# Two-layer diffusion trunk on one core: where mask additions and a modulation part stand, and how many chunks go stream by stream

## The chip, the cores and the metric

The kernel runs on one core of a Trainium2 chip. The metric is the device time of one execution in microseconds (us); less is better. The core's engines each run their own fixed instruction stream: TensorE (PE in the profile, its weight loads PEld), VectorE (DVE), ScalarE (ACT), GpSimd (POOL) and SyncE (SP), which here only issues DMAs. An engine waits at an instruction until the semaphores it names have arrived, and everything behind that instruction on the engine waits with it.

## The reference

512 tokens of width 1024, 256 of them context and 256 latent (a grid of 4 rows by 64), go through two layers, all in fp32. Cut to what matters here:

```python
mod = silu(c) @ w_ada[l] + b_ada[l]          # 6 parts: sh1, sc1, gt1, sh2, sc2, gt2 (latent; the same for context)
h = rms_norm(x, g_attn[l]) * (1 + sc1) + sh1
p = h @ w_in[l]                              # gates | c_q (768) | c_kv (256) | k_r (32) | neighbourhood q, k, v
mq = rms_norm(rms_norm(c_q) @ w_uq)          # 8 heads of 96; the last 32 are rotated (rope_2d)
kv = rms_norm(c_kv) @ w_ukv                  # 8 heads of 64 + 64
mk = rms_norm([k_nope, k_r]);  the k_r part is rotated
y_mla = softmax(mq mk') mv                   # latent queries over context + latent, context over context
y_na  = softmax(nq nk' + bias)               # 8 x 16 windows of the grid with rpb, and all context keys
x = x + gt1 * (sigmoid(g1) * (y_mla @ w_mla_o) + sigmoid(g2) * (y_na @ w_na_o)) @ w_out[l]
h2 = rms_norm(x, g_mlp[l]) * (1 + sc2) + sh2
x = x + gt2 * (relu(h2 @ w_ff1[l]) ** 2 @ w_ff2[l])
```

The output is the latent stream; so the second layer updates the latent tokens alone.

## The kernel before

**Products.** Every fp32 product is made of three TensorE products of values rounded to fp32r: `mm3` (L100 to L103) multiplies the high part of the weights with the high and with the low part of the activations (L101 and L102 or L103), and the low part of the weights with the high one. A weight block comes by DMA from SP's queue into one of five `raw` tiles (`wraw`, L116 to L122); `wsplit` (L124 to L129) makes `whi` of it on ACT (L127) and `wlo` on DVE (L128), into one of three pairs of tiles. `proj_a` (L131) takes the output features in chunks of 128: split, 24 matmuls over all 512 tokens, evacuation (`evac`), and then `step()`. `proj_tail` (L150) is for the last chunks of a product: it splits the weights of all of them, and then does the tokens of one stream (256 columns) for each chunk, and then the other stream's, so that the norm that follows can begin with the stream that is done first. In both `hook` is called ahead of each k of the eight.

**Modulation.** `ada_side` (L233) computes parts of the modulation without TensorE: a part `(l, j, zs)` is column block j of layer l's `w_ada` for the vectors zs. For each of 8 blocks of 128 rows it loads 512 KB (the `raw` ring, SP's queue) and adds the rows, times silu(c), into accumulators on DVE (L246 for the first block, L248 for the others: two vectors of 1024 columns, in halves of 512 in the part of layer 0's attention). Then come transposes and reductions on DVE, one small matmul and the biases. It is a generator; it stands in the list `side`, and `step(n)` (L163) advances it by n pieces. Part (0,2) is the first gate of layer 0. `step(2)` (L685), the evacuation of the w_uq product (L719), that of the w_ukv product (L737), and `step(99)` (L750), which does all that is left, advance it. The list of layer 0's feed-forward (L1232) begins with part (0,5) and is advanced by that block's chunks.

**Norms.** `rms_a` (L306): one column of sums by TensorE (L311), eps added by DVE (L316), and a power on POOL (L177) that gives `rt`. `rms_b` (L321) spreads it over the partitions (TensorE, L324). `norm_apply` (L330) then does one k of 8: DVE `u` (L334), ACT high part (L338), DVE low part (L340). `last_product` (L1068) is w_out of layer 0 (then norm 2) and the last eighth of w_ff2 of layer 0 (then norm 1 of layer 1): 6 chunks by `proj_a`, 2 by `proj_tail`, with `rms_a` for the first stream ahead of (1, 1, 0), that is second stream, second chunk, k 0, and its norm ahead of (1, 1, 5). The second stream's norm is in `ff1_hook` (L1119; ahead of the first stream's second and third chunk) and, at the start of layer 1, in `ckv_hook` (L515; k 4 and k 7 of the first c_kv product).

**Attention's preparation.** The w_uq product (three groups of heads) is evacuated by ACT into `mq` (L715) and its squares summed (L597); the w_ukv product into `mk` and `mv`. POOL then has in program order: `q_stat` (L694 and others), `k_stat` (L707 and the power L177), `k_fin` (to L745) for four blocks of tokens, and `q_fin` (L697), which scales the context queries' last 32 columns (L702) and rotates the latent ones by `rope` (L607 to L617). TensorE goes on with the gates (L756): 6 chunks in layer 0 and 8 in layer 1, and then transposes queries (L775) and keys (L780) for the first head. `prep_na` (L790) loads for each head of the neighbourhood part a bias tile by 4 DMAs on SP's queue (L809) and adds the mask to it on POOL (L810); there are three such tiles in layer 0 and four in layer 1.

**The order** on each engine is fixed when the kernel is built, by a list scheduler that takes what is ready by its model, by priority of program position: what stands later in the program can be hoisted ahead (mask additions and modulation pieces among it). `keep_in_program_order` pins an instruction. `tc.issue_after(i)` places what is traced in its block behind i on the same engine; it adds no semaphore.

Of the kernel before, what the change touches and what calls it, by code (L numbers as in the profile page):

```python
# [45 lines left out]
def trunk(ctx: ExitStack, tc, t):  # L46
# [186 lines left out]
    def ada_side(parts, acc):  # L233


        for l, j, zs in parts:
            accs = [acc(z) for z in zs]
            for k in range(KD):
                raw = wraw(t["w_ada"][l], k, 1, j * D, D)[:, 0]
                for z, tiles in zip(zs, accs):  # L240
                    sc = silu[:, k, z:z + 1]
                    c = 0
                    for a in tiles:
                        w = a.shape[-1]
                        if k == 0:
                            nc.vector.tensor_scalar(out=a, in0=raw[:, c:c + w], scalar1=sc, scalar2=None, op0=ALU.mult)  # L246
                        else:
                            nc.vector.scalar_tensor_tensor(out=a, in0=raw[:, c:c + w], scalar=sc, in1=a,  # L248
                                                           op0=ALU.mult, op1=ALU.add)
                        c += w  # L250
                yield
# [78 lines left out]
    def norm_apply(k, xT, R, A, SH, hh, hl, streams, half=False):  # L330

        u = sp.tile([128, TT], F32, tag="tmp", name="u", bufs=NTMP)
        for s, c in streams:
            nc.vector.scalar_tensor_tensor(out=u[:, c], in0=xT[:, k, c], scalar=A[:, k, s:s + 1],  # L334
                                           in1=R[:, :c.stop - c.start] if half else R[:, c],
                                           op0=ALU.mult, op1=ALU.mult)
        for s, c in streams:
            nc.scalar.activation(out=hh[:, k, c], in_=u[:, c], func=AF.Identity, bias=SH[:, k, s:s + 1])  # L338
        for s, c in streams:
            nc.vector.scalar_tensor_tensor(out=hl[:, k, c], in0=u[:, c], scalar=SH[:, k, s:s + 1],  # L340
                                           in1=hh[:, k, c].bitcast(F32), op0=ALU.add, op1=ALU.subtract)

# [114 lines left out]
    for l in range(DEPTH):  # L457
# [57 lines left out]
        def ckv_hook(k):  # L515

            if k == 4:
                nxt.append(rms_a(nxt[2], both[1][1], "C", True))
            if k == 7:
                nxt[3](1, rms_b(*nxt[4], True))  # L520
# [86 lines left out]
        def rope(z, tab, lt, n):  # L607
# [8 lines left out]
            for i in range(2):  # L616
                nc.gpsimd.tensor_tensor(out=zz[:, :, :, i], in0=aa[:, :, :, i], in1=bb[:, :, :, 1 - i], op=ALU.add)  # L617
# [63 lines left out]
        if l == 0:  # L681
            block_sum()
            side.append(ada_side(((0, 2, (0, 1)),), lambda z: [ap.tile([128, TT], F32, tag="P", name="ada", bufs=4)
                                                               for _ in range(2)]))
            step(2)  # L685
# [11 lines left out]
        def q_fin(tk):  # L697
            z = mq[:, tk, :, NOPE:QK]
            if tk >= 2:
                rope(z, ropeq[:, l], tk - 2, NH)  # L700
            else:
                nc.gpsimd.tensor_tensor(out=z, in0=z, in1=gqr[:, l, :].unsqueeze(1).to_broadcast([128, NH, RD]),  # L702
                                        op=ALU.mult)
# [8 lines left out]
        for h0, n in ((0, 3), (3, 3), (6, 2)):  # L712
            def evac(tk, o):
# [5 lines left out]
                if tk % 2:  # L719
                    step()  # L720
# [29 lines left out]
        step(99)  # L750
        for tk in range(4):
            k_fin(tk)
        for tk in range(q0, 4):
            q_fin(tk)

        gates(NG0[l], "B")  # L756

# [32 lines left out]
        def prep_na(hp):  # L790
# [12 lines left out]
            for h in (2 * hp, 2 * hp + 1):  # L803
                bias = ap.tile([128, 2, ROWS, GW], F32, tag="bias", name="bias", bufs=3 + l)
                for row in range(ROWS):
# [4 lines left out]
                nc.gpsimd.tensor_tensor(out=bias.rearrange("p a i j -> p (a i) j"),  # L810
                                        in0=bias.rearrange("p a i j -> p (a i) j"),
                                        in1=wmask.unsqueeze(1).to_broadcast([128, 2 * ROWS, GW]), op=ALU.add)
# [255 lines left out]
        def last_product(w, k0, moves, gate, acc, then):  # L1068
# [12 lines left out]
            def hook(s_, i, k):  # L1081

                if (s_, i, k) == (1, 1, 0):
                    Rs.append(rms_a(acc, both[0][1], "D", True))
                if (s_, i, k) == (1, 1, 5):
                    then(rms_b(*Rs[0], True))

            proj_a(w, k0, KD, 0, 6, moves, loc, res_add(gate, sq))
            proj_tail(w, k0, (6, 7), moves, both, ev, hook)
# [20 lines left out]
        def norm_2(i, R):  # L1110
            for k in range(KD):
                norm_apply(k, xT, R, A2[l], SH2, mh, ml, [streams[i]], True)
# [3 lines left out]
                          gained if last else lambda R: norm_2(0, R))  # L1116
        R2 = []

        def ff1_hook(f):  # L1119

            if f == 1:
                R2.append(rms_a(Rs, both[1][1], "C", True))
            if f == 2:
                norm_2(1, rms_b(*R2[0], True))
# [12 lines left out]
        def ff1(g):  # L1137
# [21 lines left out]
            if g == 0 and not last:  # L1159
# [3 lines left out]
                for s_, c in both:  # L1163
                    for f, (o, (h, lo)) in enumerate(zip(os, hls)):
                        if s_ == 0:
                            ff1_hook(f)
                        for k in range(KD):
                            mm3(o[:, c], h[:, k], lo[:, k], mh[:, k, c], ml[:, k, c], k == 0, k == KD - 1)
# [8 lines left out]
        def ff2(g, a):  # L1177
            if g == 3:
# [3 lines left out]
                def norm_1(i, R):  # L1182
                    for k in range(KD):
# [3 lines left out]
                                   lambda R: norm_1(0, R))  # L1187
# [44 lines left out]
        if l == 0:  # L1232
            side.append(ada_side(((0, 5, (0, 1)), (1, 1, (0, 1)), (1, 0, (0, 1)), (1, 2, (1,)), (1, 4, (1,)),
                                  (1, 3, (1,)), (1, 5, (1,))), acc_g))
# [67 lines left out]
```

## Time and profile before

| | |
|---|---|
| device time, median of 3 runs | 1317.09 us (1316.2 to 1318.02) |
| profiled execution, its own time | 1316.76 us |
| span of that execution in the trace | 1315.0 us (1.76 us lie around it) |
| mean granted TensorE clock | 0.992 of full speed |
| PE busy | 1276.4 us, 97% |
| DVE busy | 903.5 us, 69% |
| ACT busy | 582.6 us, 44% |
| POOL busy | 269.7 us, 21% |

Times are microseconds from the start of the span. A row names start, duration, engine, line, operation, tiles out and in, shape and count; the bracket behind it is the idle time of the engine ahead of it and what released it. "SPq" is a DMA issue on SP's queue.

### The profile page before, as it was taken

To read this page: it belongs to the slowest core of one execution; us is meant where nothing else is said; L and a number is where in the kernel's file an instruction comes from. 1 tells how busy PE (TensorE), PEld (TensorE's weight loads), DVE (VectorE), ACT (ScalarE), POOL (GpSimd) and SP (SyncE) were. 2 spreads that over 40 slices of the span, in tenths; PEclk is the share of its full clock that TensorE was granted. 3 is DMA by queue.
4 is the path that set the end of the run, shared out by engine and by line. 5 is a ranking of instruction groups with operands and counts; after the bars stand their busy time and mean duration, and the time that the engine had idled before them with its cause. 6 is when DMAs were issued, how large, how long until landed. Compare 5 with 4: busy or idle time off the path is not lost.

```text
span 1315.0 us, 20278 instructions
## 1 busy us (share of the span) xinstructions
PE 1276.4 (97%) x7783; PEld 1094.9 (83%) x7783; DVE 903.5 (69%) x1545; ACT 582.6 (44%) x1052; POOL 269.7 (21%) x283
## 2 busy tenths in 40 slices
PE   7989999999999999999999999989999999999997
PEld 5788888986787898888888888889889789999896
DVE  4588387758985597997775665756763967665553
ACT  4445376446423334322323313455654545554452
POOL 0325501421004003210201100038122112121011
PEclk9999999999999999999999999999999999999999
DMA  9865500544495336566675572476214657656652
GB/s 290 298 147 148 174 17 17 180 134 57 114 321 182 114 111 179 169 182 195 205 224 176 160 224 85 120 176 182 77 49 113 134 171 211 175 159 194 192 183 90
DMA packets 241857, 208.01 MB, mean 158 GB/s; under 512 B 24464, under 2 KB 220816, under 8 KB 241376
## 3 DMA queue, kind: packets, MB, share of 16 engines
q1 hardware_dynamic: 231728, 190.16, 50.3%
q10 hardware_dynamic: 9520, 16.29, 3.5%
q8 instruction: 61, 1.00, 0.3%
q0 software_dynamic: 512, 0.27, 0.1%
q14 instruction: 36, 0.29, 0.1%
HBM read 195.15 MB, written 11.53 MB: 157 GB/s over the span
## 4 chain that ended last, share of the span: by engine, by line
PE 55%; DVE 3%; DMA 2%; ACT 1%; POOL 1%; issue 1%; POOLq 0%; ACTq 0%; DVEq 0%
PE psB L101 7%; PE psB L103 7%; PE psB L102 7%; PE psA L103 6%; PE psA L101 6%; PE psA L102 6%; PE psC L103 4%; PE psC L101 4%; PE psC L102 4%; PE psC L865 1%; DVE wlo L128 1%; PE psD L885 1%; ACT whi L127 1%; DMA raw<-in_w_uq_dram 1%; DMA bias<-in_rpb_dram 1%
## 5 line engine op out<-in xcount | busy, mean ns | idle before, releaser
L128 DVE TENSOR_TENSOR wlo<-raw,whi 128x1024 fp32r<-128x1024 f32 (+3 forms) x252 | 308.5, 1226 | 190.9 <-ACT whi L127 185.4
L127 ACT ACTIVATE whi<-raw 128x1024 fp32r<-128x1024 f32 (+3 forms) x252 | 260.4, 1035 | 364.1 <-PE psB L102 113.8
L248 DVE SCALAR_TENSOR_TENSOR ada<-raw,silu,ada 128x1024 f32<-128x1024 f32 (+1 forms) x126 | 153.1, 1245 | 25.5 <-DMA raw<-in_w_ada_dram 25.2
L102 PE MATMUL psA<-wlo,h 128*128 128x256 f32 (+2 forms) x408 | 121.1, 297 | 2.5 <-DVE wlo L128 2.5
L101 PE MATMUL psA<-whi,h 128*128 128x256 f32 (+2 forms) x408 | 120.8, 296 | 1.2 <-ACT h L338 1.1
L103 PE MATMUL psA<-whi,h 128*128 128x256 f32 (+2 forms) x408 | 120.9, 296 | 0.0
L101 PE MATMUL psB<-h,whi 128*128 128x512 f32 (+1 forms) x288 | 99.1, 345 | 0.1
L103 PE MATMUL psB<-h,wlo 128*128 128x512 f32 (+1 forms) x288 | 99.0, 344 | 0.0
L102 PE MATMUL psB<-h,whi 128*128 128x512 f32 (+1 forms) x288 | 99.0, 344 | 0.0
L101 PE MATMUL psA<-h,whi 128*128 128x512 f32 (+1 forms) x248 | 87.8, 355 | 0.8 <-ACT h L338 0.8
L103 PE MATMUL psA<-h,wlo 128*128 128x512 f32 (+1 forms) x248 | 87.3, 352 | 0.0
L102 PE MATMUL psA<-h,whi 128*128 128x512 f32 (+1 forms) x248 | 87.1, 351 | 0.0
L102 PEld LDWEIGHTS psA<-wlo,h 128*128 128x128 f32 x408 | 78.4, 192 | 5.6 <-DVE wlo L128 3.1
L101 PEld LDWEIGHTS psA<-whi,h 128*128 128x128 f32 x408 | 78.1, 192 | 3.4 <-ACT h L338 1.6
L103 PEld LDWEIGHTS psA<-whi,h 128*128 128x128 f32 x408 | 78.2, 192 | 1.9
L1156 POOL TENSOR_TENSOR fl<-s,fa 128x512 fp32r<-128x512 f32 (+1 forms) x32 | 36.2, 1130 | 167.0 <-ACT fa L1155 167.0
L101 PE MATMUL psC<-G,whi 128*128 128x258 f32 (+2 forms) x216 | 69.2, 321 | 0.3 <-ACT G L338 0.3
L102 PE MATMUL psC<-G,whi 128*128 128x258 f32 (+2 forms) x216 | 69.1, 320 | 0.2
L103 PE MATMUL psC<-G,wlo 128*128 128x258 f32 (+2 forms) x216 | 68.8, 319 | 0.2 <-DVE wlo L128 0.2
L1156 POOL TENSOR_TENSOR h<-s,h 128x512 fp32r<-128x512 f32 (+1 forms) x32 | 34.5, 1077 | 168.3 <-ACT h L1155 150.0
L102 PEld LDWEIGHTS psB<-h,whi 128*128 128x128 f32 x288 | 54.6, 190 | 6.8 <-issue 0.8
L101 PEld LDWEIGHTS psB<-h,whi 128*128 128x128 f32 x288 | 54.6, 190 | 6.9 <-issue 0.4
(389 smaller groups left out, 3323.7 us busy)
## 6 DMA issues: line engine op xcount, KB each, us to landing
raw<-in_w_ff_dram SPq DMA_DIRECT2D x128, 512.0 KB, 4.1
raw<-in_w_ada_dram SPq DMA_DIRECT2D x80, 512.0 KB, 4.1
raw<-in_w_in_dram SPq DMA_DIRECT2D x62, 512.0 KB, 3.7
raw<-in_w_out_dram SPq DMA_DIRECT2D x16, 512.0 KB, 4.5
spare<-in_w_ada_dram SPq DMA_DIRECT2D x12, 512.0 KB, 8.6
xT_d<-xT SPq DMA_DIRECT2D x2, 2048.0 KB, 10.2
bias<-in_rpb_dram SPq DMA_DIRECT2D x64, 64.0 KB, 7.0
g_d<-g ACTq DMA_DIRECT2D x16, 256.0 KB, 4.4
```

Source lines behind the costliest of these rows:

```text
L101: nc.tensor.matmul(out, sh, mh, start=first, stop=False)
L102: nc.tensor.matmul(out, sh, ml, start=False, stop=False)
L103: nc.tensor.matmul(out, sl, mh, start=False, stop=last)
L127: nc.scalar.activation(out=hi, in_=src, func=AF.Copy)
L128: nc.vector.tensor_tensor(out=lo, in0=src, in1=hi.bitcast(F32), op=ALU.subtract)
L248: nc.vector.scalar_tensor_tensor(out=a, in0=raw[:, c:c + w], scalar=sc, in1=a, op0=ALU.mult, op1=ALU.add)
L865: nc.tensor.transpose(o[:, kt * 256 + i * 128:kt * 256 + (i + 1) * 128], pt[:, (kp * 2 + kt) * 128:(kp * 2 + kt + 1) * 128], perm if K == ...
L885: mm = nc.tensor.matmul(yo[z * 64:(z + 1) * 64, oc], vsel(kt, 2 * hp + z), tr[kt // 2][:, kt % 2, :], start=kt == nkt - 1, stop=kt == 0, t ...
L1156: nc.gpsimd.tensor_tensor(out=al[:, f, :], in0=s[:, :TQ], in1=ah[:, f, :].bitcast(F32), op=ALU.subtract)
```

## The change

- **Mask additions.** The addition of the mask to a bias tile (L810, both layers) is placed on POOL behind `q_end`, the last operation of the last query block's `q_fin`.
- **Modulation (0,2).** `step(2)` and the step in the w_uq evacuation go. The part is advanced by the w_ukv evacuations, by the gates' chunks, and the rest by `step(99)`, which now stands behind the gates.
- **Modulation (0,5) and those after it.** The first of these operations (L246) is placed on DVE behind the last operation of norm 2 of the second stream (`behind`, a function that gives that instruction).
- **Last products of layer 0.** 5 chunks by `proj_a` and 3 by `proj_tail`; `rms_a` ahead of (1, 0, 7); k 0 to 4 of the first stream's norm ahead of (1, 1, 4), and k 5 to 7 after the tail.
- **Second stream's norms.** `ckv_hook` at k 3 and 6 in place of 4 and 7; in ff1 `rms_a` ahead of (1, 0) as before and the norm ahead of (1, 5), in place of (2, 0).

```diff
-    def ada_side(parts, acc):
+    def ada_side(parts, acc, behind=None):
...
+                lead, behind = behind, None
...
                         if k == 0:
-                            nc.vector.tensor_scalar(out=a, in0=raw[:, c:c + w], scalar1=sc, scalar2=None, op0=ALU.mult)
+                            with tc.issue_after(lead()) if lead else nullcontext():
+                                nc.vector.tensor_scalar(out=a, in0=raw[:, c:c + w], scalar1=sc, scalar2=None,
+                                                        op0=ALU.mult)
...
-            if k == 4:
+            if k == 3:
                 nxt.append(rms_a(nxt[2], both[1][1], "C", True))
-            if k == 7:
-                nxt[3](1, rms_b(*nxt[4], True))
+            if k == 6:
+                nxt[3](1, rms_b(*nxt[4], True), range(KD))
...
             side.append(ada_side(((0, 2, (0, 1)),), lambda z: [ap.tile([128, TT], F32, tag="P", name="ada", bufs=4)
                                                                for _ in range(2)]))
-            step(2)
...
                 if h0 == 6:
                     q_stat(tk)
-                if tk % 2:
-                    step()
...
-        step(99)
         for tk in range(4):
             k_fin(tk)
         for tk in range(q0, 4):
-            q_fin(tk)
+            q_end = q_fin(tk)
 
         gates(NG0[l], "B")
+        step(99)
...
-                nc.gpsimd.tensor_tensor(out=bias.rearrange("p a i j -> p (a i) j"),
-                                        in0=bias.rearrange("p a i j -> p (a i) j"),
-                                        in1=wmask.unsqueeze(1).to_broadcast([128, 2 * ROWS, GW]), op=ALU.add)
+                with tc.issue_after(q_end.ins):
+                    nc.gpsimd.tensor_tensor(out=bias.rearrange("p a i j -> p (a i) j"),
+                                            in0=bias.rearrange("p a i j -> p (a i) j"),
+                                            in1=wmask.unsqueeze(1).to_broadcast([128, 2 * ROWS, GW]), op=ALU.add)
...
-                if (s_, i, k) == (1, 1, 0):
+                if (s_, i, k) == (1, 0, 7):
                     Rs.append(rms_a(acc, both[0][1], "D", True))
-                if (s_, i, k) == (1, 1, 5):
-                    then(rms_b(*Rs[0], True))
-
-            proj_a(w, k0, KD, 0, 6, moves, loc, res_add(gate, sq))
-            proj_tail(w, k0, (6, 7), moves, both, ev, hook)
+                if (s_, i, k) == (1, 1, 4):
+                    then(rms_b(*Rs[0], True), range(0, 5))
+
+            proj_a(w, k0, KD, 0, 5, moves, loc, res_add(gate, sq))
+            proj_tail(w, k0, (5, 6, 7), moves, both, ev, hook)
+            then(Rs[0][0], range(5, 8))
             return acc
...
-        def ff1_hook(f):
-
-            if f == 1:
+        def ff1_hook(f, k):
+
+            if (f, k) == (1, 0):
                 R2.append(rms_a(Rs, both[1][1], "C", True))
-            if f == 2:
-                norm_2(1, rms_b(*R2[0], True))
+            if (f, k) == (1, 5):
+                R2.append(norm_2(1, rms_b(*R2[0], True), range(KD)))
...
-                                  (1, 3, (1,)), (1, 5, (1,))), acc_g))
+                                  (1, 3, (1,)), (1, 5, (1,))), acc_g, lambda: R2[1].ins))
```

## Rows read from the trace of the kernel before

**Rows 1.** The page's first part: busy time, share of the span and instructions of each engine.

```profile
PE 1276.4 (97%) x7783; PEld 1094.9 (83%) x7783; DVE 903.5 (69%) x1545; ACT 582.6 (44%) x1052; POOL 269.7 (21%) x283
```

**Rows 2.** Windows: from:to, length, busy us (instructions) of PE, PEld, DVE, ACT and POOL, granted PE clock, DMA share, GB/s. They are the w_uq product of layer 0, the end of layer 0's w_ff2 with the start of layer 1's c_kv, the w_uq product of layer 1, and a stretch in the attention.

```profile
88.40:99.10 10.70, 5.50 (x24) 5.06 (x23) 10.70 (x17) 3.80 (x8) 0.43 (x1) 0.68 0.49 153
831.00:847.00 16.00, 13.74 (x86) 12.67 (x86) 12.97 (x33) 7.37 (x16) 0.70 (x1) 0.89 0.59 197
880.10:891.00 10.90, 6.70 (x31) 6.42 (x31) 5.45 (x8) 5.95 (x11) 1.93 (x2) 0.69 0.66 190
245.00:248.00 3.00, 1.56 (x13) 1.36 (x12) 3.00 (x5) 1.49 (x3) 0.00 (x0) 1.00 0.78 210
```

**Rows 3.** Timeline of PE in the w_uq product of layer 0.

```profile
90.24 0.40 PE L101 MATMUL psA<-whi,G 128*128 128x288 f32 x1 [1.40 <-ACT mqk L715]
...
94.44 0.61 PE L102 MATMUL psB<-wlo,G 128*128 128x288 f32 x1 [3.80 <-DVE wlo L128]
```

**Rows 4.** Timeline of DVE in the same stretch.

```profile
91.35 2.06 DVE L248 SCALAR_TENSOR_TENSOR ada<-raw,silu,ada 128x512 f32<-128x512 f32 x3
...
93.33 2.02 DVE L128 TENSOR_TENSOR wlo<-raw,whi 128x864 fp32r<-128x864 f32 x2
```

**Rows 5.** Timeline of SP's queue ahead of it: loads of w_ada and of w_uq.

```profile
81.02 9.39 SPq L118 DMA_DIRECT2D raw<-in_w_ada_dram  x2
...
93.44 1.40 SPq L118 DMA_DIRECT2D raw<-in_w_uq_dram  x2
```

**Rows 6.** Timeline of POOL in layer 1, from a mask addition in the w_uq product to the last operation on the keys.

```profile
880.56 1.26 POOL L810 TENSOR_TENSOR bias<-bias,wmask 128x512 f32<-128x512 f32 x1 [6.28 <-DMA bias<-in_rpb_dram]
881.78 0.71 POOL L177 TENSOR_TENSOR rt<-ms,mhalf 128x2 f32<-128x2 f32 x1
...
892.05 0.74 POOL L613 TENSOR_TENSOR ro<-mqk,ropeq 128x256 f32<-128x256 f32 x1 [9.56 <-ACT mqk L715]
...
899.17 0.88 POOL L617 TENSOR_TENSOR mqk<-ro 128x128 f32<-128x128 f32 x2
...
906.65 1.04 POOL L745 TENSOR_TENSOR mqk<-mqk,krz 128x512 f32<-128x512 f32 x1
...
923.02 1.04 POOL L745 TENSOR_TENSOR mqk<-mqk,krz 128x512 f32<-128x512 f32 x1
```

**Rows 7.** Timeline of PE beside the first two rows of that.

```profile
883.98 0.39 PE L101 MATMUL psB<-whi,G 128*128 128x192 f32 x1 [3.79 <-ACT whi L127]
...
884.77 0.53 PE L102 MATMUL psB<-wlo,G 128*128 128x192 f32 x1 [0.41 <-DVE wlo L128]
```

**Rows 8.** Timeline of PE at the first head's transposes of the keys (four in a row), layer 0 and layer 1.

```profile
158.42 0.60 PE L780 MATMUL psC<-ident,mqk 128*96 128x128 f32 x4
...
925.92 0.60 PE L780 MATMUL psC<-ident,mqk 128*96 128x128 f32 x4
```

**Rows 9.** Timeline of POOL in layer 0, from the context queries to the last operation on the keys.

```profile
110.51 2.65 POOL L702 TENSOR_TENSOR mqk<-mqk,gqr 128x256 f32<-128x256 f32 x1 [21.68 <-ACT sq L597]
...
116.17 0.85 POOL L694 TENSOR_SCALAR qrs<-qrs,rt 128x8 f32<-128x8 f32 x1
116.98 0.73 POOL L702 TENSOR_TENSOR mqk<-mqk,gqr 128x256 f32<-128x256 f32 x1
...
119.82 0.27 POOL L694 TENSOR_SCALAR qrs<-qrs,rt 128x8 f32<-128x8 f32 x1
...
149.83 1.04 POOL L745 TENSOR_TENSOR mqk<-mqk,krz 128x512 f32<-128x512 f32 x1
```

**Rows 10.** Groups by line, every shape apart: the mask additions (busy us, mean ns; then idle time ahead of them and what ended it).

```profile
L810 POOL TENSOR_TENSOR bias<-bias,wmask 128x512 f32<-128x512 f32 x16 | 22.5, 1404 | 162.0 <-DMA bias<-in_rpb_dram 109.3 <-DMA g_d<-g 32.0 <-DVE ada L259 11.0
```

**Rows 11.** Timeline of DVE beside POOL's row at 116.17, and of POOL beside DVE's row at 480.90 (Rows 15).

```profile
115.66 1.23 DVE L128 TENSOR_TENSOR wlo<-raw,whi 128x1024 fp32r<-128x1024 f32 x1 [0.82 <-ACT whi L127]
...
481.06 1.68 POOL L177 TENSOR_TENSOR rt<-ms,mhalf 128x2 f32<-128x2 f32 x1 [10.85 <-DVE ms L316]
```

**Rows 12.** Timeline of PE at the end of layer 0's w_ff2 and the start of layer 1's c_kv.

```profile
837.93 0.40 PE L102 MATMUL psA<-wlo,h 128*128 128x288 f32 x1 [0.64 <-DVE wlo L128]
...
842.19 0.40 PE L101 MATMUL psA<-whi,h 128*128 128x288 f32 x1 [1.11 <-ACT h L338]
```

**Rows 13.** Timeline of DVE in the same stretch: evacuations of the tail's chunks (half of the tokens each).

```profile
825.18 0.48 DVE L1057 SCALAR_TENSOR_TENSOR xT<-psC,modT,xT 128x256 f32<-128x256 f32 x1 [1.37 <-PE psC L103]
...
828.01 0.48 DVE L1057 SCALAR_TENSOR_TENSOR xT<-psA,modT,xT 128x256 f32<-128x256 f32 x1 [1.43 <-PE psA L103]
...
836.74 0.48 DVE L1057 SCALAR_TENSOR_TENSOR xT<-psB,modT,xT 128x256 f32<-128x256 f32 x1
```

**Rows 14.** Timeline of PE at the end of layer 0's w_out: the spread of the first stream's norm.

```profile
482.79 0.71 PE L324 MATMUL psC<-ident,rt 128*128 128x128 f32 x4 [0.86 <-POOL rt L177]
```

**Rows 15.** Timeline of DVE there and in ff1's first chunks: modulation pieces, and the split for ff1's chunk 3.

```profile
480.90 1.28 DVE L248 SCALAR_TENSOR_TENSOR ada<-raw,silu,ada 128x1024 f32<-128x1024 f32 x1
...
491.04 2.48 DVE L248 SCALAR_TENSOR_TENSOR ada<-raw,silu,ada 128x1024 f32<-128x1024 f32 x2
...
494.11 1.22 DVE L128 TENSOR_TENSOR wlo<-raw,whi 128x1024 fp32r<-128x1024 f32 x1
```

**Rows 16.** Timeline of ACT in layer 0's gates: the splits of two chunks that follow one another (all 512 tokens each).

```profile
141.63 1.06 ACT L127 ACTIVATE whi<-raw 128x1024 fp32r<-128x1024 f32 x1 [3.90 <-PE psB L102]
147.08 1.06 ACT L127 ACTIVATE whi<-raw 128x1024 fp32r<-128x1024 f32 x1 [3.90 <-PE psB L102]
```

## What the change will do to the time

> **What bounds the kernel now.** I read the page's first part first: TensorE is busy 97% of the span [rows 1], so only what it idles, or does at a low clock, can be won. Then the windows over the places that the change touches. In layer 0's w_uq product 5.50 us of 10.70 are busy and the granted clock is 0.68; at the end of w_ff2 13.74 of 16.00, clock 0.89; in layer 1's w_uq product 6.70 of 10.90, clock 0.69 [rows 2]. A mean below 1 is a stretch at 1.2 GHz in place of 2.4, so a stall costs its gap and the slow matmuls behind it. The clock's part can't exceed its shortfall times the window: 3.4, 1.8 and 3.4 us. Last I read the timeline of TensorE for the gaps and what released them, and those of POOL, DVE and SP's queue, whose order the change edits.
>
> **Layer 0's w_uq stall goes.** TensorE waits 1.40 and 3.80 us, the second time for `wlo` [rows 3]. DVE is late with it because three modulation operations, 2.06 us, stand ahead of the two splits [rows 4], and the weights were late in turn: SP's queue issues two w_ada loads, 9.39 us, ahead of w_uq's [rows 5]. The gaps are 5.2 us. The 24 matmuls [rows 2] need some 3.2 us at full speed (24 matmuls of 256 columns take 828.01 - 825.18 = 2.83 [rows 13], times 288/256) and are busy 5.50: another 2.3 is clock. 7.5 altogether. Without `step(2)` and the uq steps neither load nor operation stands here. What is late next is the evacuation on ACT, the 1.40, of which half may remain. I take **-7.5 + 0.7 = -6.8**, bounds -7.5 and -4.
>
> **Where that modulation goes.** Eight pieces of four DVE operations, 0.69 us each (2.06 for three [rows 4]): 22 us, beside the 48 us of TensorE's work from 110.51 to the keys' transposes at 158.42 [rows 8, 9]. DVE has room: a chunk of gates asks for one split of 1.23 us [rows 11] in 147.08 - 141.63 = 5.45 us [rows 16]. The question is POOL, which works on the queries and keys in that stretch. It ends at 149.83 + 1.04 = 150.87 [rows 9], and the fourth transpose, which needs the last block, comes at about 158.8 (the four begin at 158.42 [rows 8]): 7.9 us to spare. DVE and POOL hold each other up: POOL's L694, otherwise 0.27, takes 0.85 beside a split that had begun 0.51 earlier [rows 9, 11], and L177 takes 1.68 beside a modulation operation of 1.28 [rows 11, 15], where it took 0.71 elsewhere [rows 6]. Each time POOL lost about the rest of DVE's operation. But L702 takes 2.65 against 0.73 [rows 9], more than the rest of any one operation on DVE here.
>
> The Trainium skill, "SBUF — State Buffer", section "SBUF: two separate sides", says that DVE and POOL share a pair of ports under an exclusive lock, whichever starts first, for a whole instruction. The two rows at 116.17 and 481.06 agree with it; if a hand-over then never cost more than one operation, the sum below would stand, and the row at 110.51 says that it can cost more, which is rival D.
>
> Five loads fit the ring of `raw` and share it with the gates' weights, so I put six of the eight pieces, 24 operations, into POOL's work. If each costs half its length, 0.35, POOL loses 8.3; if four in ten do, 3.5; at the row of 2.65 it loses nearly their whole time, 16.6. The mask additions move there too: three tiles of 1.404 us [rows 10], 4.2 us, between `q_end` and the keys' operations. That leaves 3.7 to spare against 3.5 to 8.3, and the pieces of `step(99)` lay in the same stretch before, so part of the price is in the 150.87 already. I take **0**, bounds 0 and +7 (a gap of 4.6 and 2.3 of clock as in w_uq).
>
> **Layer 1's w_uq stall goes.** POOL sits 6.28 us at the mask addition of 880.56, for a bias DMA, and the power that the evacuation needs stands behind it at 881.78 [rows 6]; TensorE waits 3.79 and 0.41 [rows 7]. 4.2 of gaps, and nearly all of the clock's 3.4, say 3.2. Placed behind `q_end` the addition no longer stands there: **-7.4**, bounds -7.4 and -5 (ACT's own evacuations, as in layer 0).
>
> **But the additions come back.** `q_end` in layer 1 is the L617 that ends at 899.17 + 0.88 = 900.05 [rows 6]. Four bias tiles are free, so four additions, 5.6 us [rows 10], may run there; the one at 880.56 had its data 20 us earlier. Program order has `q_fin` behind `k_fin`, yet this L617 ran 7 us ahead of the first L745, at 906.65 [rows 6]: the list takes what is ready. So I expect the additions, too, ahead of the keys. From 892.05 to 924.06 POOL has no idle time in its rows [rows 6], so every microsecond is passed on. The keys' transposes begin at 925.92, the fourth at about 926.3 [rows 8]: 2.2 to spare, and 5.6 - 2.2 = 3.4. The queries' evacuations come earlier with the stall gone, but TensorE's transposes do as well, so the slack stays within a few tenths. I take **+3.2, and +2.3 for a low clock behind it**; bounds 0 and +7. The clock could stay full: in the stretch from 245 TensorE idled nearly half of 3 us at a clock of 1.00 [rows 2], while the gaps of 3.8 had a low clock behind them [rows 2, 3, 7]. Net for this layer **-1.9**.
>
> **The end of w_ff2 and c_kv.** Gaps of 0.64 and 1.11 [rows 12], smaller ones of 0.5, and 1.7 of the clock's 1.8: 4.0. The reason is order on DVE: the last evacuation, 836.74, comes 8.7 us after the one at 828.01 [rows 13] since the first stream's norm runs between, so `rms_a` of the second stream is late. With three chunks by stream the first stream is done a chunk earlier, and three k of its norm come after the tail. One more chunk in halves costs 2 x 2.83 against 5.45 whole [rows 13, 16], +0.2 to +0.3. All three pairs of split tiles are then held by the tail, so the next product's weights can't be split before it ends: I leave 1.0 of waiting. **-4.0 + 0.3 + 1.0 = -2.7**, bounds -4 and +1.
>
> **The end of w_out and ff1.** A gap of 0.86 [rows 14] and 0.8 in smaller ones: 1.65, no low clock. The first hangs on the power that took 1.68 beside a modulation operation [rows 11, 15]; with (0,5) behind norm 2 that is gone. The same 0.3 for halves. But the pieces taken from here come bunched behind the norm: six operations of 1.28, 7.7 us, ahead of the split for ff1's chunk 3, which even before had two of them, 2.48, in front of it and came at 494.11 [rows 15]. I take +1.3 for this (bounds 0 and 5, a gap of 3 with clock). **-1.65 + 0.3 + 1.3 = 0**.
>
> **Sum** against the profiled execution, 1316.76 us (the span of 1315.0 and 1.76 around it; the median lies 0.33 higher): -6.8 + 0 - 1.9 - 2.7 + 0 = -11.4, or 1305.4. I say **1305.5**.
>
> **Rivals.**
>
> *A, the forecast*, 0.50; 1301 to 1310 by its small terms.
>
> *B, the additions find room in layer 1*, 0.22. The list puts them behind `k_fin`, or between the power's waits. For it: their priority is lower than the keys'. Against it: `q_end` itself ran early [rows 6]. It saves 3.2 + 2.3 and up to 0.7 in layer 0: 1299, 1296.5 to 1302.
>
> *C, the moved modulation delays layer 0's keys*, 0.15: A plus 4 to 7 us of gap and clock: 1312, 1308 to 1316. For it: additions and modulation together take 7.7 to 12.5 of 7.9. Against it: the pieces of before, already paid.
>
> *D, slower: POOL is starved under layer 0's gates.* The mechanism is that of L702 at 110.51 [rows 9], where POOL got no turn between DVE's operations. If the pieces run back to back, POOL loses 17 to 22 us, and 4.2 for the additions; less 7.9 that is 13 to 18 of gap, and 2.3 of clock: 1321 to 1326, say 1323.5. It breaks even at about 9 us of gap, that is when POOL loses some 13 us beyond the additions. 0.13. The skill's rule above, if it means a turn for each engine, speaks against it.
>
> **How the numbers follow.** A holds the largest chance, so its value is the time. Left out of the range are the low end of B (0.04), the top of C (0.03) and D (0.13): 1297.5 to 1314. 0.2%, 2.6 us, is about what a measurement of this kernel can tell from no change. Faster by more: A, B and 0.06 of C, 0.78. Within: 0.08, of C and of D's lower side. Slower: 0.14, D and the worst of C.
>
> **What would show it.** In layer 0's w_uq no gap over 1.4 us and a clock near 1. Under its gates L248, with POOL's small operations lengthened by one DVE operation (A, C) or by several (D), and the last L745 before or after TensorE reaches L780. In layer 1 the power of w_uq without an addition in front, then L810 four times between L617 and the first L745, a gap of some 3 us at L780, and a low clock behind it. At w_ff2's end an earlier `rms_a`, and a first matmul of c_kv that waits for `whi` or `wlo`. In ff1 a wait for `wlo` behind L248. I am wrong if the additions stand behind `k_fin` (B), if L780 of layer 0 waits over 5 us (C, D), or if w_ada's loads, now beside the gates' weights on SP's queue, open a wait there that no term above has.

## The result, and the profile after

The changed kernel takes 1333.49 us (median of 4 runs, 1329.63 to 1334.41), the one before 1316.64 on the same chip: 1.0122 times as long, interval 1.0100 to 1.0145. The forecast was 1305.5, with 1297.5 to 1314 as its range: wrong in direction.

The profiled execution took 1333.42 us, its span 1331.6, that is 16.6 more than before. The page's first part hardly differs [rows 1]:

```profile
PE 1274.8 (96%) x7831; PEld 1095.6 (82%) x7831; DVE 905.8 (68%) x1547; ACT 582.6 (44%) x1054; POOL 271.2 (20%) x283
```

So the work is the same, and the time lies in gaps of TensorE and in its clock. Windows of the changed kernel (columns as in [rows 2]): layer 0's w_uq and w_ukv in two parts, ff1's start, layer 1's w_ukv up to the keys' transposes in two, and c_kv of layer 1.

```profile
100.60:116.02 15.42, 12.01 (x80) 10.53 (x78) 12.19 (x20) 5.13 (x11) 3.07 (x3) 1.00 0.66 195
116.02:133.09 17.07, 5.15 (x11) 3.64 (x12) 11.33 (x19) 3.59 (x8) 14.48 (x19) 0.50 0.36 107
508.55:515.38 6.83, 3.09 (x7) 2.48 (x8) 6.83 (x6) 1.20 (x2) 1.57 (x1) 0.50 0.50 144
903.40:938.63 35.23, 29.63 (x222) 28.04 (x221) 20.90 (x29) 19.20 (x35) 33.64 (x38) 1.00 0.73 209
938.63:945.46 6.83, 5.15 (x22) 4.83 (x23) 0.79 (x2) 1.07 (x2) 1.63 (x3) 0.50 0.07 24
855.00:859.00 4.00, 3.23 (x23) 2.69 (x22) 2.42 (x8) 1.22 (x3) 0.70 (x1) 1.00 1.02 301
```

In the places that the change touches, three stretches run at a clock of 0.50 (1.2 GHz), and each begins in a long idle time of TensorE; a fourth, shorter one lies in a place that no part touches, near 1095. As the clock's loss I count half of TensorE's busy time in such a stretch: 5.15 / 2 = 2.57, 3.09 / 2 = 1.55, 5.15 / 2 = 2.57. That is an estimate and a little too much: the same matmul of 256 columns comes every 0.12 us at 932 and every 0.21 at 941. With the gaps from TensorE's timeline that makes, place by place:

| Place | loss before | forecast of the difference | loss after | measured difference |
|---|---|---|---|---|
| w_uq and w_ukv, layer 0 | 1.40 + 3.80 + 2.3 = 7.5 | -6.8 | 0.83 + 7.61 + 6.89 + 2.57 = 17.9 | +10.4 |
| keys' transposes, layer 0 | 0 | 0 | 0 | 0 |
| w_uq to the keys, layer 1 | 3.79 + 0.41 + 3.2 = 7.4 | -1.9 | 1.58 + 0.69 + 5.01 + 2.57 = 9.9 | +2.5 |
| end of w_ff2 and c_kv | 4.0 | -2.7 | 0.32 + 0.45 = 0.8 | -3.2 |
| end of w_out and ff1 | 1.65 | 0 | 0.31 + 0.56 + 0.45 + 1.52 + 4.96 + 1.55 = 9.4 | +7.7 |
| sum | | -11.4 | | +17.4 (span +16.6) |

**Layer 0.** The w_uq stall [rows 3] is gone; a larger one stands in w_ukv. Timelines of PE and of DVE:

```profile
121.05 0.80 PE L102 MATMUL psB<-wlo,G 128*128 128x512 f32 x1 [7.61 <-DVE wlo L128]
129.16 0.79 PE L101 MATMUL psB<-whi,G 128*128 128x512 f32 x1 [6.89 <-ACT mv L735]
```

```profile
111.05 2.74 DVE L251 SCALAR_TENSOR_TENSOR ada<-raw,silu,ada 128x512 f32<-128x512 f32 x4 [1.53 <-DMA raw<-in_w_ada_dram]
...
117.12 2.74 DVE L251 SCALAR_TENSOR_TENSOR ada<-raw,silu,ada 128x512 f32<-128x512 f32 x4 [2.81 <-DMA raw<-in_w_ada_dram]
119.78 1.22 DVE L128 TENSOR_TENSOR wlo<-raw,whi 128x1024 fp32r<-128x1024 f32 x1
125.61 0.75 DVE L251 SCALAR_TENSOR_TENSOR ada<-raw,silu,ada 128x512 f32<-128x512 f32 x1 [4.62 <-DMA raw<-in_w_ada_dram]
...
128.46 1.21 DVE L128 TENSOR_TENSOR wlo<-raw,whi 128x1024 fp32r<-128x1024 f32 x1
```

TensorE waits for `wlo` at 119.78. Ahead of it on DVE stand modulation pieces, and DVE sits idle at them, 1.53 and 2.81 us, for a load of w_ada; then the evacuation of w_ukv (its first copy comes at 128.13) stands behind one more wait, of 4.62. The pieces are still in w_uq and w_ukv, not under the gates: DVE begins with them at 87.03, the rows at 111.05 and 117.12 are the sixth and the seventh of the eight, and by program order even the first is traced behind w_ukv's first evacuations. SP's queue shows why their loads are late:

```profile
109.55 0.38 SPq L118 DMA_DIRECT2D raw<-in_w_in_dram  x1
113.82 0.33 SPq L118 DMA_DIRECT2D raw<-in_w_ada_dram  x1
119.89 0.38 SPq L118 DMA_DIRECT2D raw<-in_w_in_dram  x1
121.02 0.33 SPq L118 DMA_DIRECT2D raw<-in_w_ada_dram  x1
```

Loads of w_ada and of the gates' weights alternate, each waiting for one of the five `raw` tiles: between 100 and 131 us SP waited 13.0 us for low splits on DVE and 6.7 for modulation operations there. A tile is free when DVE has read it, DVE waits for the load, and the load takes over 3 us (113.82 to 117.12): engine and queue wait for each other in turn.

**Layer 1.** POOL, and PE beside it:

```profile
909.19 4.79 POOL L813 TENSOR_TENSOR bias<-bias,wmask 128x512 f32<-128x512 f32 x3
...
915.20 1.30 POOL L813 TENSOR_TENSOR bias<-bias,wmask 128x512 f32<-128x512 f32 x1
916.44 2.64 POOL L177 TENSOR_TENSOR qrs<-qrs,mhalf 128x8 f32<-128x8 f32 x1
...
939.22 1.04 POOL L747 TENSOR_TENSOR mqk<-mqk,krz 128x512 f32<-128x512 f32 x1
```

```profile
905.03 0.50 PE L101 MATMUL psA<-whi,G 128*128 128x512 f32 x1 [1.58 <-ACT mv L735]
...
934.99 0.31 PE L782 MATMUL psC<-ident,mqk 128*96 128x128 f32 x1 [0.69 <-POOL mqk L747]
940.31 0.45 PE L782 MATMUL psC<-ident,mqk 128*96 128x128 f32 x1 [5.01 <-POOL mqk L747]
```

No addition waits in w_uq any more [rows 6, 7]. Four additions stand right behind the rotation, 4.79 + 1.30 us of POOL's chain, and TensorE waits for the last block of keys. That is the stall that the forecast had, only longer.

**ff1 and w_ff2.** PE and DVE at ff1's chunk 3, and PE at the start of c_kv [rows 12]:

```profile
506.60 0.50 PE L101 MATMUL psA<-G,whi 128*128 128x512 f32 x1 [1.52 <-ACT whi L127]
...
512.29 0.79 PE L103 MATMUL psB<-G,wlo 128*128 128x512 f32 x1 [4.96 <-DVE wlo L128]
...
856.52 0.71 PE L327 MATMUL psC<-ident,rt 128*128 128x128 f32 x4 [0.32 <-POOL rt L177]
...
858.34 0.40 PE L101 MATMUL psA<-whi,h 128*128 128x288 f32 x1 [0.45 <-ACT h L341]
```

```profile
501.27 1.28 DVE L251 SCALAR_TENSOR_TENSOR ada<-raw,silu,ada 128x1024 f32<-128x1024 f32 x1
502.47 1.29 DVE L1159 TENSOR_TENSOR s<-r 128x512 f32<-128x512 f32 x2
503.67 3.49 DVE L251 SCALAR_TENSOR_TENSOR ada<-raw,silu,ada 128x1024 f32<-128x1024 f32 x2
507.08 1.75 DVE L1159 TENSOR_TENSOR s<-r 128x512 f32<-128x512 f32 x1
508.76 1.27 DVE L251 SCALAR_TENSOR_TENSOR ada<-raw,silu,ada 128x1024 f32<-128x1024 f32 x1
509.95 2.28 DVE L128 TENSOR_TENSOR wlo<-raw,whi 128x1024 fp32r<-128x1024 f32 x1
```

The pieces are bunched ahead of the split at 509.95, which TensorE waits for until 512.29; before, two of them stood there [rows 15]. Operations that take 1.28 alone take 1.75 on average in the pair at 503.67, and the split 2.28 in place of 1.22: POOL's subtractions for ff1's first chunks run beside them (from 503.95 and from 509.57).

### The profile page after: what moved, and what is told of

It reads as the page before. It is cut to its first block, busy times and chain, and to the rows that moved or that the text cites. A ratio compares the mean times of both kernels' runs of the same rounds, so it can differ in the third digit from the quotient of the medians.

```text
span 1331.6 us, 20386 instructions
## 1 busy us (share of the span) xinstructions
PE 1274.8 (96%) x7831; PEld 1095.6 (82%) x7831; DVE 905.8 (68%) x1547; ACT 582.6 (44%) x1054; POOL 271.2 (20%) x283
## 4 chain that ended last, share of the span: by engine, by line
PE 49%; DVE 3%; POOL 3%; DMA 3%; issue 2%; ACT 1%; SPq 0%; POOLq 0%; ACTq 0%; DVEq 0%
PE psB L101 6%; PE psB L103 6%; PE psB L102 6%; PE psA L103 6%; PE psA L101 6%; PE psA L102 6%; PE psC L103 4%; PE psC L101 4%; PE psC L102 4%; DVE wlo L128 1%; ACT whi L127 1%; DMA raw<-in_w_na_o_dram 1%; DMA raw<-in_w_ukv_dram 1%; PE psD L888 1%; DMA bias<-in_rpb_dram 1%
## 5 line engine op out<-in xcount | busy, mean ns | idle before, releaser
L128 DVE TENSOR_TENSOR wlo<-raw,whi 128x1024 fp32r<-128x1024 f32 (+3 forms) x252 | 313.2, 1244 | 183.1 <-ACT whi L127 181.9
L101 PE MATMUL psB<-h,whi 128*128 128x256 f32 (+1 forms) x272 | 91.8, 338 | 0.1
L102 PE MATMUL psB<-h,whi 128*128 128x256 f32 (+1 forms) x272 | 91.8, 338 | 0.0
L103 PE MATMUL psB<-h,wlo 128*128 128x256 f32 (+1 forms) x272 | 91.7, 337 | 0.0
L103 PE MATMUL psB<-G,wlo 128*128 128x512 f32 (+2 forms) x192 | 67.1, 349 | 5.3 <-DVE wlo L128 5.3
L101 PE MATMUL psB<-G,whi 128*128 128x512 f32 (+2 forms) x192 | 67.1, 349 | 0.0
L102 PE MATMUL psB<-G,whi 128*128 128x512 f32 (+2 forms) x192 | 66.9, 348 | 0.0
L101 PE MATMUL psC<-G,whi 128*128 128x258 f32 (+2 forms) x200 | 62.5, 313 | 0.0
L102 PE MATMUL psC<-G,whi 128*128 128x258 f32 (+2 forms) x200 | 62.5, 312 | 0.0
```

Source lines behind the costliest of these rows:

```text
L101: nc.tensor.matmul(out, sh, mh, start=first, stop=False)
L102: nc.tensor.matmul(out, sh, ml, start=False, stop=False)
L103: nc.tensor.matmul(out, sl, mh, start=False, stop=last)
L128: nc.vector.tensor_tensor(out=lo, in0=src, in1=hi.bitcast(F32), op=ALU.subtract)
```

## The experiments

The theory: the loss has three separate places, each from where the list puts moved work (pieces and their loads ahead of w_ukv's low splits; additions ahead of the keys; pieces ahead of ff1's low split), and the three chunks by streams are a gain. The rival for layer 0 is the forecast's own case D, POOL starved.

**One part alone, four kernels.** Each is the kernel before with one part of the change's diff, and nothing else.

```diff
 mod_only: part (0,2) not stepped in step(2) and w_uq; step(99) behind the gates
 mask_only:  with tc.issue_after(q_end.ins): (mask addition)
 behind_only: ada_side(..., acc_g, lambda: R2[1].ins)
 tails_only: proj_a 5 chunks, proj_tail (5, 6, 7), the hooks' new places
```

> The kernel before with the move of modulation part (0,2) alone. Theory: the pieces are hoisted ahead of w_ukv's second low split on DVE, and each waits there for a w_ada load that in turn waits for a free raw tile; in layer 0 TensorE then has the two gaps of 7.6 and 6.9 us and the low clock of the changed kernel without any other edit: about 1327 us beside 1316.6 (1324 to 1330). Rival (the mask additions are needed for the stall, since POOL is what holds the chain): 1310 to 1317 and no gap at w_ukv.

Measured 1327.64 beside 1316.53 (1.0088, 1.0071 to 1.0104): +11.1. The gaps at w_ukv are those of the changed kernel:

```profile
122.21 0.79 PE L102 MATMUL psB<-wlo,G 128*128 128x512 f32 x1 [7.74 <-DVE wlo L128]
...
130.45 0.80 PE L101 MATMUL psB<-whi,G 128*128 128x512 f32 x1 [7.03 <-ACT mv L735]
```

No mask addition was moved, so the rival falls.

> The kernel before with the mask additions behind the queries' rotation alone. Theory: layer 1 loses its w_uq stall (7.4 us) and gets a stall of about 5 us at the keys' transposes, 0.7 and 1.6 us more, and a low clock: +1 to +2.5, so 1317.5 to 1319; layer 0 nothing, as its chain has 7.9 us to spare. Rival (the additions cost 3.2 + 2.3, as forecast): 1314.7.

1317.79 beside 1316.53 (1.0014, 1.0003 to 1.0025): +1.3. In layer 1 the gaps are 0.69 and 5.01 with half of 2.78 busy at 1.2 GHz behind them, 7.1 against the 7.4 that went. A gain of nothing there, as the theory had it. The +1.3 is the sum of that with changes for which this part has no term: layer 0's w_uq has gaps of 0.36 and 2.88 in place of 1.40 and 3.80, and near 1076 there are 2.72 us of gaps with a granted clock of 0.66 (1074 to 1084), in place of 2.25 at full clock. So single microseconds of a kernel's total can't be put down to one place.

> The kernel before with the modulation from part (0,5) on placed behind norm 2 alone. Theory: the pieces come bunched ahead of the low split of ff1's chunk 3, TensorE waits 4 to 6.5 us and has a low clock there, and 1 us is won at w_out: +4 to +7, so 1320.5 to 1323.5. Rival (the wait comes from the three chunks by streams, which hold all three pairs of split tiles): 1315 to 1317.

1323.24 beside 1316.53 (1.0052, 1.0032 to 1.0071): +6.7. PE of this kernel at ff1's chunk 3:

```profile
496.39 0.50 PE L101 MATMUL psB<-G,whi 128*128 128x512 f32 x1 [2.21 <-ACT whi L127]
...
502.14 0.80 PE L103 MATMUL psC<-G,wlo 128*128 128x512 f32 x1 [5.01 <-DVE wlo L128]
```

The wait is there with two chunks by streams as well: it isn't the held split tiles.

> The kernel before with the three chunks by streams and the earlier hooks alone. Theory: 3 us won at the end of w_ff2, 0 to 1 at w_out: 1312.5 to 1314. Rival (three chunks by streams make ff1 wait for its split): 1316 to 1320.

1306.91 beside 1316.53 (0.9927, 0.9913 to 0.9940): -9.6, three times what was expected. At c_kv 3.2 us are won as in the changed kernel. Most of the rest lies in a place that this part doesn't touch, layer 1's w_uq (some 1.5 more in layer 0's, with gaps of 0.51 and 3.92 and 3.4 us at 1.2 GHz in place of 6.8). POOL of this kernel:

```profile
871.26 1.30 POOL L815 TENSOR_TENSOR bias<-bias,wmask 128x512 f32<-128x512 f32 x1 [4.76 <-DMA bias<-in_rpb_dram]
872.52 0.71 POOL L177 TENSOR_TENSOR rt<-ms,mhalf 128x2 f32<-128x2 f32 x1
880.35 1.29 POOL L815 TENSOR_TENSOR bias<-bias,wmask 128x512 f32<-128x512 f32 x1 [7.13 <-DMA bias<-in_rpb_dram]
```

Here the list placed the last of the additions, which waits 7.13 us, behind the power and not ahead of it [rows 6], so the stall of 7.4 us is gone without any ordering of the additions; w_ukv has a gap of 2.2 and the keys 0.6.

The four differences add up to +9.5, and the whole change has +16.9. So two parts must win the same thing:

> Three chunks by streams and the earlier hooks, with the mask additions behind the queries' rotation as in the change. Theory (both of them remove the same w_uq stall of layer 1, and the additions' place brings the stall at the keys back): 1306.9 + 6 = 1313 (1311 to 1315). Rival (the two add up, -9.6 and +1.3): 1308.

```diff
 tails_only, and
+                with tc.issue_after(q_end.ins):
```

1312.43 beside 1315.63 (0.9972, 0.9961 to 0.9983): -3.2, where the sum of the two is -8.3. The gaps at the keys are 0.69 and 5.01 again. 5 of the 7.4 us that were not additive are this. The other 2 were not followed up; they may be layer 0's w_uq, where mask_only and tails_only lost less than the kernel before, and where the moved part takes the stall away in any case.

**Layer 0: the wait for loads, or DVE's work?**

> The kernel before with the move of part (0,2) alone, as mod_only, but all eight pieces of that part read the rows that the first piece loaded: seven loads of w_ada are left out (the part's values are then others), the 32 operations on DVE stay in the same place among the low splits. Theory (DVE waits there for loads that wait for raw tiles): the two gaps of 7 us at w_ukv shrink to 0 to 2 us in all: 1310 to 1314. Rival (the operations themselves, some 9 us of DVE time in a row ahead of the split, are the delay): gaps of 8 us or more stay, 1320 to 1328.

```diff
-                raw = wraw(t["w_ada"][l], k, 1, j * D, D)[:, 0]
+                if (l, j) != (0, 2) or k == 0:
+                    raw = wraw(t["w_ada"][l], k, 1, j * D, D)[:, 0]
```

1317.55 beside 1315.63 (1.0007, 0.9995 to 1.0018): +1.9 where mod_only has +11.1, so 9.2 less, between the two expectations. PE and DVE of this kernel:

```profile
116.15 0.50 PE L102 MATMUL psB<-wlo,G 128*128 128x512 f32 x1 [2.64 <-DVE wlo L128]
...
118.71 0.80 PE L101 MATMUL psB<-whi,G 128*128 128x512 f32 x1 [1.71 <-ACT mv L736]
```

```profile
105.61 8.83 DVE L252 SCALAR_TENSOR_TENSOR ada<-raw,silu,ada 128x512 f32<-128x512 f32 x13
...
114.89 1.21 DVE L128 TENSOR_TENSOR wlo<-raw,whi 128x1024 fp32r<-128x1024 f32 x1
```

Both were partly right. Without the loads DVE has no idle time there, but 13 operations in a row, 8.83 us, still stand ahead of the split and cost 2.64 + 1.71 and a low clock (5.12 busy in 6.83 us, so 2.56); with a gap of 0.50 in w_uq that is 7.4 us of loss in this place against 17.9 in the changed kernel. Some 10 are the waits for loads (with the clock that follows them), some 7 the operations' place. Leaving out the loads also leaves the raw tiles to others, so the split between the two is not exact.

**Layer 0: the pieces where the forecast had them.**

> The kernel before with modulation part (0,2) moved, and its first operation placed on DVE behind the last sum of squares of the w_ukv evacuation, so that all its pieces run under the gates, as the forecast had pictured. Theory (what the change lost in layer 0 is the place of the pieces, ahead of w_ukv's low splits, not their work under the gates): no stall in w_uq and none in w_ukv: 1310.5 beside 1316.5 (1308.5 to 1313.5). Rival (POOL starves under the gates, or the loads hold the raw tiles that the gates' weights need): a gap at the gates or at the keys' transposes, 1318 or more.

```diff
 mod_only, w_ukv's evacuation without step(), and
-                                                               for _ in range(2)]))
+                                                               for _ in range(2)], lambda: kss[-1].ins))
```

1313.51 beside 1316.57 (0.9980, 0.9965 to 0.9995): -3.1. Windows of this kernel, from w_uq to the gates; then the last row of modulation pieces on DVE, and POOL and PE at the end of the keys:

```profile
88.00:150.00 62.00, 62.00 (x347) 54.61 (x347) 47.20 (x70) 28.57 (x54) 45.34 (x49) 1.00 0.58 173
```

```profile
139.64 9.57 DVE L251 SCALAR_TENSOR_TENSOR ada<-raw,silu,ada 128x512 f32<-128x512 f32 x12
```

```profile
148.62 1.49 POOL L746 TENSOR_TENSOR mqk<-mqk,krz 128x512 f32<-128x512 f32 x1
```

```profile
158.99 0.61 PE L781 MATMUL psC<-ident,mqk 128*96 128x128 f32 x4
```

TensorE is busy for all of the 62 us. POOL ends at 150.11, late by what DVE took from it, and still 9 us ahead of the keys. So the stretch can be had as the forecast pictured it, without a stall at w_uq, at w_ukv or at the keys; the changed code did not make it. This run both ties the pieces and takes the steps out of w_ukv's evacuation; the two were not tried apart. The whole of the 7.5 isn't won: 2.4 us of gaps stand later (0.3 to 1.3 each between 150 and 182), for `wlo`, and for the first head's queries behind two splits on DVE.

> The changed kernel with one edit: part (0,2)'s first operation stands on DVE behind the last sum of squares of the w_ukv evacuation. Theory (layer 0's stall is 18 us of the changed kernel's time, 2 of which come back at the gates): 1333.5 - 16 = 1317.5 (1315 to 1320). Rival (layer 0's chain on POOL, now with the additions too, runs out of its 7.9 us and stalls the keys' transposes): 1322 or more.

```diff
 the changed kernel, w_ukv's evacuation without step(), and
-                                                               for _ in range(2)]))
+                                                               for _ in range(2)], lambda: kss[-1].ins))
```

1320.26 beside 1315.63 (1.0037, 1.0025 to 1.0049): +4.6 where the changed kernel has +16.9, so 12 less, and a little outside 1315 to 1320. 4.6 us of loss are left behind the keys (gaps of 0.71, 1.32, 0.51 and 0.33, and the clock). Here the additions stand in POOL's chain of layer 0 too; POOL and PE of this kernel:

```profile
118.87 4.76 POOL L812 TENSOR_TENSOR bias<-bias,wmask 128x512 f32<-128x512 f32 x3
...
155.91 1.04 POOL L746 TENSOR_TENSOR mqk<-mqk,krz 128x512 f32<-128x512 f32 x1
```

```profile
159.54 0.61 PE L781 MATMUL psC<-ident,mqk 128*96 128x128 f32 x4
```

POOL ends at 156.95, 2.6 us ahead of the transposes. So case D's mechanism doesn't reach TensorE even with both in the chain.

**The additions, and ff1's pieces, in other places.**

> The kernel before with the mask additions placed behind the last operation on the keys (k_fin) in place of the queries' rotation. Theory: layer 1's w_uq stall of 7.4 us goes and nothing comes back at the keys' transposes: 1309.5 (1308 to 1311.5). Rival (the return of the stall has another cause than the additions' place, or the additions are now late for the neighbourhood part): 1314 to 1318.

```diff
-                with tc.issue_after(q_end.ins):
+                with tc.issue_after(k_end[0].ins), tc.issue_after(k_end[1].ins):   # both operations of the last k_fin
```

1312.30 beside 1316.57 (0.9962, 0.9947 to 0.9976): -4.3. The return at the keys is gone; POOL and PE of this kernel:

```profile
919.48 1.04 POOL L750 TENSOR_TENSOR mqk<-mqk,krz 128x512 f32<-128x512 f32 x1
920.48 6.09 POOL L817 TENSOR_TENSOR bias<-bias,wmask 128x512 f32<-128x512 f32 x4
```

```profile
920.57 0.32 PE L786 MATMUL psC<-ident,mqk 128*96 128x128 f32 x1 [0.58 <-POOL mqk L750]
```

In layer 1, 1.0 us of 7.4 is left. The time gains 2 us less than that: the stretch near 1075, which no part touches, lost 4.8 us here and 2.25 before.

> The kernel before with the modulation from part (0,5) on placed on DVE behind the low split of ff1's first whole chunk, and not advanced by the three chunks by streams. Theory (ff1 waits only since the pieces stand ahead of that split): the 9 us of stall there are gone, 1 us is won at w_out: 1315 to 1316. Rival (w_ada's loads ahead of w_ff1's on SP's queue make it wait anyway): 1319 to 1323.

```diff
-                    ev(f, o)
-                    step()
+                    ev(f, o)
 ...
+ (1, 5, (1,))), acc_g, lambda: splits[-1].ins))   # the low split of chunk 3
```

1318.06 beside 1316.57 (1.0015, 1.0002 to 1.0027): +1.5, worse than the theory had. ff1 is free of stalls (0.45 is left of 9.4), but the modulation is later all along the block, and at the end of w_ff2 TensorE waits 1.51 us for a reduction of it and 1.33 for a power: 7.5 us of loss there in place of 4.0.

> Three chunks by streams and the earlier hooks (1306.9 alone), with the mask additions behind k_fin and the modulation from part (0,5) on behind the low split of ff1's first whole chunk. Theory: in layer 1 the three chunks alone had already lost the w_uq stall, so the additions' place gives 0.6 at most, and w_out 1: 1305 to 1306.5. Rival (the gains add up, 9.6 and 7): 1300.

The edits of tails_only, mask_kfin and ff1_late together: 1308.29 beside 1316.57 (0.9940, 0.9925 to 0.9955). No better than tails_only alone; 6.3 us are lost at the end of w_ff2, as in ff1_late.

> Three chunks by streams with the earlier hooks, the mask additions behind k_fin, and part (0,2) behind w_ukv's evacuation; the modulation from (0,5) on as before the change. Theory: no stall in w_uq in either layer, none at the keys, none at ff1, 3 us won at the end of w_ff2: 1306.9 - 6 + 2 - 2 = 1301 (1298.5 to 1303.5). Rival (the three edits shift the list's order against one another): 1305 or more.

The edits of tails_only, mask_kfin and mod_ukv together: 1305.88 beside 1315.63 (0.9926, 0.9913 to 0.9939). It beats both kernels and is not told apart from tails_only (1306.91, measured beside other runs). The expected 1301 was missed: in layer 0 5 us of small gaps and clock have taken the place of w_uq's 6.

## Why the prediction was wrong

**The step that failed** is "Where that modulation goes", with the sentence of the section ahead of it, "Without `step(2)` and the uq steps neither load nor operation stands here". The program's position was read as the place on the engine. The list placed the pieces ahead of it. SP's queue and DVE of the changed kernel:

```profile
80.55 9.24 SPq L118 DMA_DIRECT2D raw<-in_w_ada_dram  x2
90.42 0.38 SPq L118 DMA_DIRECT2D raw<-in_w_ukv_dram  x1
```

```profile
87.03 0.49 DVE L248 TENSOR_SCALAR ada<-raw,silu 128x512 f32<-128x512 f32 x1 [4.08 <-DMA raw<-in_w_ada_dram]
```

Two loads of w_ada go out ahead of w_ukv's second, and DVE begins with the pieces in w_uq. The section of the prediction that costs the mask additions says that "the list takes what is ready"; applied here, it gives pieces in front of w_ukv's splits. The w_uq term itself came out: 0.83 of 7.5 us is left. Loads and pieces still stand in that stretch, but behind the last load of w_uq, which goes out at 76.35 in place of 93.44 [rows 5]. What had no term is the stall at w_ukv, 7.61 + 6.89 + 2.57 = 17.1. Together the place was forecast at -6.8 and measured at +10.4; mod_only has it alone, with +11.1. The waits for loads had been named as what would make the prediction wrong, for the gates' weights, and had no price.

**Case D** had the sign and not the mechanism. Its place was POOL's chain under the gates. With the pieces really there (mod_ukv) POOL ends at 150.11, and with the additions too (after_mod_ukv) at 156.95, ahead of the transposes both times. The bound of 17 to 22 us from the one row of 2.65 was far too high. The price by half a length, 8.3 us, is near: in mod_ukv the blocks of keys follow one another, by their last operations, at 126.46, 132.76, 141.48 and 148.62, 22.2 us for three; before they had 149.83 - 133.94 = 15.9 in layer 0, so 6.3 more. The remark that part of the price is in the 150.87 already was a misreading: before, the last of the 32 operations ended at 111.43, and only the part's transposes and reductions came behind it. The Trainium skill, "SBUF — State Buffer", section "SBUF: two separate sides", says that a DVE instruction with two SBUF inputs and a POOL instruction that reads SBUF share a pair of ports, that whichever starts first has it for its whole instruction, and that the other is fully blocked. The trace agrees as far as it goes: L746 lost 0.45 us (1.49 against 1.04), less than one of the modulation operations beside it (9.57 us for twelve); no run here shows who takes which turn.

**Layer 1** went as the forecast said, step by step: the w_uq stall gone (-7.4), four additions right behind `q_end`, a stall at the keys with a low clock. It was mis-sized: 0.69 + 5.01 + 2.57 = 8.3 in place of 3.2 + 2.3. The additions take 6.09 us, near what was costed (5.6), but the power behind them took 2.64 in place of 1.65, and TensorE, free of its stall, needs the keys earlier than POOL's chain has become earlier: in mask_only the keys' transposes begin at 916.07 in place of 925.92, 9.85 us earlier, and the queries' rotation ends at 892.10 in place of 900.05, only 7.95 earlier. So of the 2.2 us to spare, for which the forecast allowed "a few tenths", 0.3 was left. That mask_kfin removes it shows the cause. 1.58 at w_ukv for `mv` had no term.

**w_out and ff1** had the mechanism and a sixth of the size. The pieces that "come bunched behind the norm", ahead of the split for ff1's chunk 3, were costed at 1.3 with 0 to 5 as bounds; it is 8.0 with the clock. Six operations of 1.28 were counted, 7.7 us; they take longer beside POOL's subtractions (1.75 each at 503.67), the chunks' squares stand between them, and the load for the next chunk lands only at 505.49 (ACT's split of it begins there), 4.1 us behind its issue at 501.39.

**The end of w_ff2** was right: -2.7 forecast, -3.2 measured. Which of the edits there wins it, the third chunk, the earlier `rms_a` or the three k after the tail, was not tried. 1.7 of it is the low clock, which mod_ukv and mod_one_load don't have either, though their gaps there are those of the kernel before (0.64, 0.39 and 1.12 in mod_ukv). That the same part changes the order of the additions on POOL in layer 1's w_uq, worth 4.6 us, was not foreseen; in the changed kernel this gain can't be seen beside the ordering, which removes the same stall.

## What to carry to other kernels

Where a list scheduler orders the engines, a piece traced later is not issued later; ask of each moved piece where it becomes ready, what it waits for there, and whose instruction stands behind it. If it has to run in a certain stretch, tie it to an instruction of that stretch, and look at the tie's far side: what is released at that point runs in one bunch ahead of whatever comes next. Try the parts of a change alone: here one part alone won 9.6 us, and the other three alone lost 19 in all.

## What the runs showed of the hardware that was not expected

DVE and POOL slow each other in both directions. In mod_ukv, with the pieces in rows under the gates, twelve modulation operations took 9.57 us, 0.80 each against 0.69 [rows 4], and a POOL operation of 1.04 (L746) took 1.49; a low split between the pieces took 1.22, as it does alone. In the last kernel (best) the slow splits come behind the pieces, beside the mask additions: two of 1024 columns took 4.29 us (148.85), 2.15 each against 1.23 alone, and three additions 5.74 (149.80), 1.91 each against 1.40 [rows 10]. Neither engine starved the other.

The length of one idle time did not foretell the clock. In mod_one_load gaps of 2.64 and 1.71 us went with 6.83 us at 1.2 GHz. In the last kernel gaps of 1.34 and 0.51, near one another at 176, were followed by 3.4 us at 1.2 GHz; mod_ukv has the same two gaps in the same place and a granted clock of 1.00 throughout. A gap of 2.20 in tails_only, at w_ukv of layer 1, had a full clock behind it.
